# The output projection as seven products over all eight token tiles, with the right blocks summed and split in stage one

## Chip, cores and metric

The kernel runs on one core of a Trainium2 chip. The metric is the device time of one execution in microseconds (us). A profile of one execution goes with it: what each engine did and when. TensorE (PE) does the matmuls, VectorE (DVE) and ScalarE (ACT) the element-wise work, GpSimd (POOL) a little of it, and SyncE's queue (SP) issues nearly all transfers (DMAs).

## What is computed

One layer of a streaming encoder: two attentions from one input projection, gated and merged, an output projection, a layer norm, a gated feed-forward network (FFN) and a second norm. Sequence and model width are 1024, the inner width of the FFN is 2816, everything is float32.

```python
h = x @ w_in[l]
qa, ka, va, qb, kb, vb, ga, gb = jnp.split(h, split_pts, axis=-1)
y_a = chunk_band_attention(heads_a(qa), heads_a(ka), heads_a(va), rel_bias[l]) @ w_proj_a[l]
y_b = stick_breaking_attention(heads_b(qb), heads_b(kb), heads_b(vb)) @ w_proj_b[l]
gate_a = jax.nn.sigmoid(ga + b_gate[l, :D])
gate_b = jax.nn.sigmoid(gb + b_gate[l, D:])
mix = (gate_a * y_a + gate_b * y_b) @ w_out[l]
x = layer_norm(DEEPNORM_ALPHA * x + mix, ln1_g[l], ln1_b[l])
gu = x @ w_ffn_in[l]
g, u = jnp.split(gu, 2, axis=-1)
ffn = (jax.nn.silu(g) * u) @ w_ffn_out[l]
x = layer_norm(DEEPNORM_ALPHA * x + ffn, ln2_g[l], ln2_b[l])
```

## The kernel before

**Products in three parts.** A float32 product a b is made of three fast products: each operand is split into a high part (ScalarE copies it into the type float32r) and a low part (VectorE subtracts the high part from it), and TensorE adds a_h b_h, a_h b_l and a_l b_h. `split` (L109, L110) does one operand, `mm3` (L116 to L119) the three matmuls. Weights are split in the same way by `begin_w` (L550, L551).

**Seven products for eight.** Most big products are cut into 2 x 2 blocks and done with seven block products, as Strassen and Winograd do, so that sums and differences of blocks have to be made of both operands. `run_pairs` runs such units, one after another, seven steps p each; a step is 12 matmuls of 128x512. It prepares the next unit's operands between the steps, calls `aside` after each step and `also` at the unit's end.

**Stages.** (1) The input projection, units 0 to 13, until 333.6 us of the profile; each unit from 6 on lasts some 19 us. `aside_work(i)` puts other work at the end of unit i + 1: `sum_wo(j)` makes four differences of the blocks of w_out (L576 to L579) and stores them to `wt_dr`; `store_proj` splits parts of the projections behind the attentions and stores them. (2) The attentions, 16 heads, until about 640 us: scores (`sc_a`, L705 and L706), a custom VectorE operation that adds the bias and takes the maximum (L748), the exponential on ScalarE (L754), a scaling on GpSimd (L759), transposes on TensorE (`tp_a`, L817), splits, and the products with v (`pv_a`). Between a head's matmuls stand matmuls that wait for nothing there, the fill: first the gate blocks 10 to 15 (`gps`, L606, 24 matmuls for each half of the tokens), then a projection. `FILL` gives their number by head, 18 in the first ones. (3) The second projection, the merge into `mA`, the output projection (`ops`), the first norm, and transposes of its result (`x1ps`, L1209). (4) The two products of the FFN, from 766.7 us on, and the second norm.

**The output projection.** Token tiles 0 to 3 go by seven products of two tiles each (L1369, 7 x 2 x 12 matmuls); tiles 4 to 7 go plainly (through `mm3`, 2 halves x 4 tiles x 24 matmuls). Its weights are loaded after the attentions, w_out's own blocks and the stored differences, and split there (`begin_wo`, 16 tiles of 128x1024). `take_in` adds a finished accumulator to the residual tile `acc` (L1348). `norm_1` is one VectorE chain but for the power: statistics (L1183), their sum (L1186), a power on GpSimd (L1187), scaling (L1188), and the second scaling with the offset ln1_b (L1191).

**What sets the order.** Each engine works through one queue in order. A scheduler of the framework sets these orders at build time from the program's order and its own estimates, but for the instructions that are tied to one another by hand. Tiles live in slots: a tag has so many buffers, and a new tile waits until the old one in its buffer is done with.

```python
SLOTS = dict(bw=9, pt=4, yt=3, qs=2, kh=2, kl=2, v=2, gt=3, kp=4, op=8, xt=16)
BANKS = dict(mm=2, sc=2, tr=3, pv=1)
```

The slots `qs`, `kh`, `kl` and `v` hold a head's queries, keys (high and low) and values during the attentions, and side work's tiles in stage one; `cycle` goes round a list of tags.

## Time and profile before

| | |
|---|---|
| median of 3 runs | 1412.12 us (1411.85 to 1412.22) |
| the profiled execution | 1412.51 us, of which the span on the core is 1410.7 |
| TensorE busy | 1399.7 us, 99%, 6642 matmuls in the trace |
| VectorE, ScalarE, GpSimd busy | 1034.1, 699.0, 236.0 us |
| DMA | 292.28 MB, share of the 16 engines 58.2% |
| granted TensorE clock | 0.999 |

A profile line of a group gives the code line, engine, operation, output and inputs, shapes and count, then the busy time in us and the mean of one in ns, then the engine's idle time before them and what ended it. A line of the chain gives a start and a duration in us and what ran. Idle time of an engine that is not the bottleneck costs nothing.

### The profile page before, as it was taken

The page shows a single profiled execution, that of the slowest core. Times are in us where ns is not written, and L with a number is a line of the kernel's source. Part 1 is how long each engine was busy: PE and PEld are TensorE (multiplying, and loading weights), DVE is VectorE, ACT ScalarE, POOL GpSimd, SP SyncE. Part 2 cuts the span into 40 slices and gives each one's busy share as a digit, 9 for nine tenths or more (in the row PEclk, how much of TensorE's full clock was granted, in tenths as well). Part 3 has the DMA queues.
Part 4 walks back from the last instruction along what each step waited for, and adds up shares of the span by engine and source line. Part 5 has one row for each costly group of instructions (what it writes and reads, how often), then busy time and mean ns, then how long its engine had stood idle before and what let it go on. Part 6 is the DMA issues. An engine that isn't in the chain of part 4 may idle for free.

```text
span 1410.7 us, 18935 instructions
## 1 busy us (share of the span) xinstructions
PE 1399.7 (99%) x6642; PEld 1164.6 (83%) x6642; DVE 1034.1 (73%) x1671; ACT 699.0 (50%) x1245; POOL 236.0 (17%) x308
## 2 busy tenths in 40 slices
PE   9999999999999999999999999999999999999997
PEld 7888888888888888888888888888888888888886
DVE  8967657545887788878998967767677765847666
ACT  6544444545888888774413644434444443322220
POOL 0000000002555878750001000000000000000033
PEclk9999999999999999999999999999999999999999
DMA  7476468856676478755651144433444349996652
GB/s 254 165 286 224 178 236 303 295 179 238 212 231 208 130 252 281 253 198 194 231 202 75 61 148 166 149 141 143 164 164 149 143 144 342 411 385 236 233 194 90
DMA packets 98927, 292.28 MB, mean 207 GB/s; under 512 B 9728, under 2 KB 26112, under 8 KB 98832
## 3 DMA queue, kind: packets, MB, share of 16 engines
q1 hardware_dynamic: 98832, 291.07, 58.2%
q8 instruction: 52, 0.85, 0.3%
q14 instruction: 43, 0.35, 0.1%
HBM read 187.20 MB, written 100.17 MB: 204 GB/s over the span
## 4 chain that ended last, share of the span: by engine, by line
PE 94%; DVE 2%; DMA 1%; ACT 1%; issue 1%; POOL 0%; DVEq 0%; SPq 0%; ACTq 0%; POOLq 0%
PE sxf L179 16%; PE d L1512 15%; PE sxp L179 9%; PE szf L179 8%; PE v L481 5%; PE gps L606 4%; PE szp L179 4%; PE syf L179 4%; PE yAps L910 3%; PE ops L1369 3%; PE syp L179 2%; PE tp_b L817 2%; PE tp_a L817 2%; PE plain L347 1%; PE pv_b L833 1%; PE pv_b L832 1%
## 5 line engine op out<-in xcount | busy, mean ns | idle before, releaser
L1512 PE MATMUL d<-wd,sl 128*128 128x512 f32 (+1 forms) x924 | 207.7, 387 | 0.0
L1512 PEld LDWEIGHTS d<-wd,sl 128*128 128x128 f32 x924 | 172.3, 188 | 35.4
L1532 POOL TENSOR_TENSOR mv<-mv,neghalf 128x1 f32<-128x1 f32 x8 | 9.0, 1121 | 606.7 <-DVE mv L1531 606.7
L109 ACT CAST wd<-wd 128x512 fp32r<-128x512 f32 x77 | 45.9, 621 | 114.1 <-PE d L1512 66.8
L794 POOL TENSOR_TENSOR w_b<-w_b,kp_b 128x511 f32<-128x511 f32 (+3 forms) x96 | 96.0, 1012 | 23.2 <-DVE kp_b L789 16.7
L110 DVE TENSOR_TENSOR sl<-h,sl 128x512 fp32r<-128x512 f32 x77 | 52.6, 686 | 27.6 <-ACT sl L109 27.6
L789 DVE TENSOR_TENSOR_SCAN kp_b<-kp_b,ident_ps 128x512 f32<-128x512 f32 (+2 forms) x64 | 56.5, 885 | 21.0 <-ACT kp_b L786 20.0
L109 ACT CAST sl<-h 128x512 fp32r<-128x512 f32 x77 | 47.5, 620 | 48.1 <-PE syf L179 18.3
L1489 DVE TENSOR_TENSOR x<-d,x 128x512 f32<-128x512 f32 (+1 forms) x41 | 27.6, 675 | 47.6 <-PE d L1512 47.5
L786 ACT ACTIVATE kp_b<-sc_b 128x512 f32<-128x512 f32 (+3 forms) x96 | 48.3, 504 | 28.0 <-PE sc_b L706 23.6
L110 DVE TENSOR_TENSOR wd<-wd,wd 128x512 fp32r<-128x512 f32 x77 | 52.7, 709 | 10.7 <-ACT wd L109 10.6
L179 PE MATMUL szf<-x1S63h,wcf 128*128 128x512 f32 x168 | 55.1, 389 | 0.0
L110 DVE TENSOR_TENSOR pt_b<-tp_b,pt_b 128x512 fp32r<-128x512 f32 (+1 forms) x96 | 49.9, 544 | 6.6 <-ACT pt_b L109 5.7
L729 POOL MEMSET bias<- 64x64 f32 x2 | 0.3, 145 | 314.3 <-ACT bias L725 314.3
L109 ACT CAST pt_b<-tp_b 128x512 fp32r<-128x512 f32 (+1 forms) x96 | 46.6, 503 | 8.0 <-PE tp_b L817 7.6
L759 POOL TENSOR_SCALAR w_a<-w_a,st_a 128x640 f32<-128x640 f32 (+2 forms) x64 | 42.2, 669 | 48.0 <-PE sc_a L706 26.6
L754 ACT ACTIVATE w_a<-w_a,st_a 128x640 f32<-128x640 f32 (+2 forms) x64 | 44.7, 700 | 8.6 <-DVE st_a L748 7.5
L787 ACT ACTIVATE w_b<-sc_b 128x511 f32<-128x511 f32 (+3 forms) x96 | 48.3, 504 | 0.0
L817 PE MATMUL tp_b<-ident,w_b 128*128 128x128 f32 x288 | 47.3, 272 | 0.2
L110 DVE TENSOR_TENSOR pt_a<-tp_a,pt_a 128x512 fp32r<-128x512 f32 (+1 forms) x96 | 44.6, 486 | 3.3 <-ACT pt_a L109 2.2
L1307 ACT ACTIVATE h<-sxf 128x512 f32<-128x512 f32 x21 | 12.6, 598 | 68.2 <-PE sxf L179 68.2
L817 PEld LDWEIGHTS tp_b<-ident,w_b 128*128 128x128 f32 x288 | 36.4, 140 | 11.1 <-DVE pt_b L110 1.1
(1574 smaller groups left out, 4285.2 us busy)
## 6 DMA issues: line engine op xcount, KB each, us to landing
s_dr<-sl SPq DMA_DIRECT2D x77, 512.0 KB, 2.6
sl<-s_dr SPq DMA_DIRECT2D x77, 512.0 KB, 7.6
wLf<-in_w_ffn_in_dram SPq DMA_DIRECT2D x22, 512.0 KB, 4.3
wRf<-in_w_ffn_in_dram SPq DMA_DIRECT2D x22, 512.0 KB, 3.6
wd<-in_w_ffn_out_dram SPq DMA_DIRECT2D x22, 512.0 KB, 8.2
v_dr<-vc SPq DMA_DIRECT2D x16, 512.0 KB, 3.4
qs<-q_dr SPq DMA_DIRECT2D x16, 512.0 KB, 6.7
kh<-k_dr SPq DMA_DIRECT2D x16, 512.0 KB, 6.5
```

The lines of the kernel that those rows point to most:

```text
L109: return (nc.scalar.copy(dst_h, src), nc.vector.tensor_tensor(dst_l, src, dst_h.bitcast(F32), ALU.subtract))
L110: nc.vector.tensor_tensor(dst_l, src, dst_h.bitcast(F32), ALU.subtract))
L179: mm(acc, lw[:, ks], rx, start=(first and kt == i == 0), stop=(kt == 3 and i == 2), skip_group_check=not first)
L481: mm(accs[j], a, b, start=(first and kt == n == 0), stop=(kt == 3 and n == 2), skip_group_check=True)
L606: mm(acc[hf], lw[:, ks], rx[k][:, (LO, HI)[hf]], start=(k == j == 0), stop=(k == KT - 1 and j == 2))
L754: nc.scalar.activation(s[:, 0:w], s[:, 0:w], AF.Exp, bias=st[:, m:m + 1], scale=-1.0, accum_out=st[:, 2:3])
L786: nc.scalar.activation(kp[:, c0:e], sc[:, 0:n], AF.Sigmoid, scale=-1.0)
L787: nc.scalar.activation(be[:, m0:e], sc[:, m0 - c0:n], AF.Sigmoid)
L789: nc.vector.tensor_tensor_scan(kp[:, 0:e], kp[:, 0:e], ident_ps()[:, 0:e], 0.0, ALU.mult, ALU.add)
L794: nc.gpsimd.tensor_tensor(be[:, m0:e], be[:, m0:e], kp[:, m0 - 1:e - 1], ALU.mult)
L817: ins = tr(tp[:, (qb - lo_q) * P:(qb - lo_q + 1) * P], wt[qb - q0][:, (kb - qb) * P:(kb - qb + 1) * P], ident)
L1512: mm(part, a, b, start=(fresh and i == k == 0), stop=(i == n - 1 and k == 2), skip_group_check=not fresh)
```

## The change

All eight token tiles go through the seven products: each of the seven (`OUT`) runs over the four tiles j of a token half, 7 x 4 x 12 matmuls. The seven sums and blocks of w_out are made for one k tile at a time by `sum_wo(kt)`, which now returns seven parts; each does at most one difference, one split and one store of 512 KB to `wo_dr`. They run one after each step of units 7, 9, 11 and 13. `store_proj` comes two at a time. After the attentions the 28 tiles are loaded already split. In the first norm, tiles 0 to 5 leave the second scaling to ScalarE, and their offset ln1_b is added by a transfer that GpSimd issues, from SBUF to SBUF, accumulating; tiles 6 and 7 stay on VectorE. The loads for the FFN's start and the stores of `x1_dr` come later, and the VectorE chain of takes, statistics, norms and some splits is tied in program order. The layout of w_out in memory changes with it, and the helpers of the two norms are merged.

The diff, cut to its core:

```diff
+    WO_AT, PROJ_AT = (6, 8, 10, 12), (5, 7, 9, 11)
+
     def aside_work(i):
         if i == 2:
             small_inputs()
-        if i in (2, 6):
-            sum_wo(i // 6)
-        if i >= len(work) - 9:
-            store_proj(i - len(work) + 9)
+        if i in PROJ_AT:
+            for j in range(2):
+                store_proj(2 * PROJ_AT.index(i) + j)
+        if i + 1 in WO_AT:
+            parts.extend(sum_wo(WO_AT.index(i + 1)))
...
-    wt_dr = {n: dram(f"wt_dr{n}_", 2) for n in ("t1", "t2", "t3", "t4")}
-    wo_src = {n: [w_out[b, j] for j in range(2)] for b, n in enumerate(("11", "12", "21", "22"))}
-
-    def sum_wo(j):
-
-        put, sub = nc.vector.tensor_tensor, ALU.subtract
-        x_, y_, z_, u_ = (cycle(QKV, f"wo{n}r{j}") for n in ("11", "12", "21", "22"))
-        for t, n in ((x_, "11"), (y_, "12"), (u_, "22"), (z_, "21")):
-            dma(t, wo_src[n][j])
-        put(x_, y_, x_, sub)
-        put(y_, u_, y_, sub)
-        put(u_, u_, x_, sub)
-        put(z_, z_, u_, sub)
-        for t, n in ((x_, "t1"), (y_, "t3"), (u_, "t2"), (z_, "t4")):
-            dma(wt_dr[n][j], t)
+    wo_dr = {p: dram(f"wo_dr{p}_", 4) for p in range(1, 8)}
+    parts = []
+
+    def next_part(i):
+        if parts:
+            parts.pop(0)()
+
+    def sum_wo(kt):
+
+        xy, zu = (cycle(("qs", "kh"), f"wo{n}r{kt}") for n in ("xy", "zu"))
+        dma(xy, w_out[kt + 4])
+        dma(zu, w_out[kt])
+        x_, y_, z_, u_ = (t[:, cs] for t in (xy, zu) for cs in (LO, HI))
+
+        def out(p, src, dst=None, in0=None, in1=None):
+            def part():
+                if dst is not None:
+                    nc.vector.tensor_tensor(dst, in0, in1, ALU.subtract)
+                o = cycle(("kl", "v"), f"wo{p}_{kt}", F32R)
+                split(o[:, LO], o[:, HI], src)
+                dma(wo_dr[p][kt], o.bitcast(F32))
+            return part
+
+        return [out(3, u_), out(1, x_), out(5, x_, x_, y_, x_), out(7, y_, y_, u_, y_),
+                out(6, u_, u_, u_, x_), out(2, z_), out(4, z_, z_, z_, u_)]
...
-              right_or_v, first=3, then=rest_of_start, also=aside_work, wide=V_AT - 1, then_right=2)
+              right_or_v, first=3, then=rest_of_start, also=aside_work, aside=next_part,
+              wide=V_AT - 1, then_right=2)
...
+    def load_wo(p):
+        wo[p] = [slot("xt", f"wo{p}_{kt}", F32R) for kt in range(4)]
+        for t, d in zip(wo[p], wo_dr[p]):
+            wo["last"] = dma(t.bitcast(F32), d)
+
+    def m_split(p, kt, src, tie=lambda ins: ins):
+        o = {5: lambda *a: slot("bw", *a), 4: lambda *a: slot("pt", *a)}.get(
+            p, lambda *a: cycle(QKV, *a))(f"m{p}_{kt}", F32R)
+        tie(split(o[:, LO], o[:, HI], src)[1])
+        m_ops[p][kt] = o
+
+    put, sub = nc.vector.tensor_tensor, ALU.subtract
+
+    def m_sums(kt):
+
+        a, b = m_raw[kt + 4], m_raw[kt]
+        m_split(4, kt, b[:, HI])
+        put(b[:, HI], a[:, HI], b[:, HI], ALU.add)
+        m_split(5, kt, b[:, HI])
+        put(a[:, HI], a[:, LO], a[:, HI], sub)
+
+    def m_sums_3(kt):
+        a, b = m_raw[kt + 4], m_raw[kt]
+        put(a[:, LO], b[:, HI], a[:, LO], sub)
+        put(b[:, LO], b[:, LO], a[:, LO], sub)
+        m_split(3, kt, b[:, LO])
 
...
+    def finish(name, n, t, g, b, lone, done, cuts=(slice(0, D),), tied=False, added=None):
...
+            if lone:
+                tie(nc.vector.scalar_tensor_tensor(t[:, cs], t[:, cs], mv[:, 2:3], b[:, cs],
+                                                   ALU.mult, ALU.add))
+            else:
+                nc.scalar.activation(t[:, cs], t[:, cs], AF.Copy, scale=mv[:, 2:3])
+                if added is None:
+                    nc.gpsimd.tensor_tensor(t[:, cs], t[:, cs], b[:, cs], ALU.add)
+                else:
+                    nc.gpsimd.dma_start(t[:, cs], added[:, cs], accum_op=ALU.add)
+            done(cs)
...
     def norm_1(tt):
+        finish(f"1_{tt}", 2, acc_t[tt], g1, b1, tt > 5, lambda cs: None, tied=True, added=b1)
+
+    bx, by = [None] * 4, [None] * 4
+
+    def project_out(p, j):
+        accs = by if p in (2, 5, 3) else bx
         first = p in (1, 2, 5)
+        if first:
+            accs[j] = bank(("tr", "tr", "tr", "pv")[j] if accs is by
+                           else ("mm", "mm", "sc", "sc")[j], f"ops{p}_{j}")
+        for kt in range(4):
+            lh, ll = (m_ops[p][kt][:, c + j * P:c + (j + 1) * P] for c in (0, HW))
+            wh, wl = (wo[p][kt][:, cs] for cs in (LO, HI))
+            for n, (a, b) in enumerate(((lh, wh), (lh, wl), (ll, wh))):
+                mm(accs[j], a, b, start=(first and kt == n == 0), stop=(kt == 3 and n == 2),
+                   skip_group_check=not first)
+        tt, cs = j + 4 * (p in (5, 7, 4)), (LO, HI)[p in (5, 7, 3, 6)]
+        take_in(tt, cs, accs[j], 1.0 if p in (2, 6, 7) else ALPHA)
+        if p in (6, 4):
+            mark(f"1_{tt}", 1, acc_t[tt][:, cs], True)
+        elif p in (2, 7):
+            mark(f"1_{tt}", 0, acc_t[tt][:, cs], p == 7)
+
+    def after_chain(work):
+        with tc.issue_after(wo["last"].ins), tc.issue_after(chained[0].ins):
+            work()
+
+    def start_of_ffn():
+        left_f(0)
+        R0 = slot("gt", "wRf0")
+        dma(R0, w_ffn_in[NF])
+        Wf[0]["hr"] = split_w(R0, "wrf0", "bw")
+
+    for p in OUT[:5]:
+        todo = {1: [lambda: m_sums(last_c), lambda: load_wo(5)], 5: [lambda: load_wo(6)],
+                2: [lambda: load_wo(3)] + [lambda kt=kt: m_sums_3(kt) for kt in range(2)],
+                3: [lambda: load_wo(7)],
+                6: []}[p]
+        if p == 5:
+            todo += [lambda kt=kt: m_sums_3(kt) for kt in (2, 3)]
+        elif p in (3, 6):
+            half = LO if p == 3 else HI
+            todo += [lambda kt=kt: m_split(6 if p == 3 else 7, kt, m_raw[kt + 4][:, half],
+                                           chain)
+                     for kt in range(4)]
+            if p == 6:
+                load_wo(4)
         elif p == 2:
             for _ in range(3):
                 more_acc("yt")
             more_acc("bw")
+        for j in range(4):
+            project_out(p, j)
+            for _ in range(-(-len(todo) // (4 - j)) if p != 6 else 2):
+                if todo:
+                    todo.pop(0)()
+            if p == 6:
+                norm_1(j)
+    for n, (p, j) in enumerate(((7, 0), (7, 1), (4, 0), (7, 2), (4, 1), (7, 3), (4, 2), (4, 3))):
+        project_out(p, j)
+        if p == 4:
+            norm_1(j + 4)
+        if n > 3:
+            x1_operands(0, acc_t, (n - 4,))
+        if n == 4:
+            after_chain(start_of_ffn)
+        elif n == 6:
+            after_chain(lambda: left_f(1))
+    for tt in range(4):
+        dma(x1_dr[tt], acc_t[tt])
+    after_chain(lambda: right_f(1))
+    after_chain(lambda: left_f(2))
 
     first_h = []
 
     def second_half():
         x1_operands(1, acc_t)
+        for tt in range(4, 8):
+            dma(x1_dr[tt], acc_t[tt])
...
```

Three places of the built orders follow. First SyncE's queue at the end of stage one, before. `qs`, `kh`, `kl` are loads for the heads, `g_dr` stores of finished gate blocks (their names end in the unit), `wp_dr` stores of `store_proj`, `braw` loads of the bias:

```order
L685 DMA qs_2626<-q_dr_77 128x1024
L720 DMA braw_2632<-rel_dr 128x640
L591 DMA wp_dr_0_291<-wh_proj_2614 128x1024
L720 DMA braw_2640<-rel_dr 128x640
L395 DMA g_dr_110<-c_12_2445 128x1024
L541 DMA wr_g_2620<-in_w_in_dram 128x1024
L395 DMA g_dr_109<-c_12_2398 128x1024
L591 DMA wp_dr_1_292<-wl_proj_2615 128x1024
L689 DMA kh_2628<-k_dr_85 128x1x1024
L685 DMA qs_2634<-q_dr_77 128x1024
L689 DMA kl_2630<-k_dr_85 128x1x1024
L689 DMA kh_2636<-k_dr_85 128x1x1024
```

And after, with `wo_dr` the stores of `sum_wo` (kt is the number 3 in the name):

```order
L590 DMA wo_dr_3_272<-wo_3_2655 128x1024
L699 DMA qs_2758<-q_dr_77 128x1024
L590 DMA wo_dr_3_280<-wo_3_2637 128x1024
L590 DMA wo_dr_3_288<-wo_3_2674 128x1024
L590 DMA wo_dr_3_296<-wo_3_2693 128x1024
L590 DMA wo_dr_3_292<-wo_3_2711 128x1024
L395 DMA g_dr_112<-c_13_2671 128x1024
L590 DMA wo_dr_3_276<-wo_3_2729 128x1024
L395 DMA g_dr_111<-c_13_2635 128x1024
L590 DMA wo_dr_3_284<-wo_3_2748 128x1024
L703 DMA kh_2760<-k_dr_85 128x1x1024
L703 DMA kl_2762<-k_dr_85 128x1x1024
```

Seven stores of the last k tile now stand ahead of the first `kh`, among them those of the parts that follow unit 13's last steps; the loads of the second head went behind.

Then TensorE's queue at the start of the attentions, before (`sxp` is unit 13's last accumulator):

```order
L179 MATMUL sxp_2513<-xl_196,wbp13h 128x512
L179 MATMUL sxp_2513<-xh_195,wbp13l 128x512
L705 MATMUL sc_a_0_0_2653<-kh_2628,qs_2626 128x320
L706 MATMUL sc_a_0_0_2653<-kl_2630,qs_2626 128x320
L705 MATMUL sc_a_0_1_2657<-kh_2628,qs_2626 128x320
L706 MATMUL sc_a_0_1_2657<-kl_2630,qs_2626 128x320
L606 MATMUL gps_0_2723<-xh_181,wh_g_2622 128x512
L606 MATMUL gps_0_2723<-xl_182,wh_g_2622 128x512
L705 MATMUL sc_a_1_0_2663<-kh_2628,qs_2626 128x320
L706 MATMUL sc_a_1_0_2663<-kl_2630,qs_2626 128x320
```

And after:

```order
L619 MATMUL gps_1_3067<-xh_195,wh_g_2754 128x512
L619 MATMUL gps_1_3067<-xl_196,wh_g_2754 128x512
L619 MATMUL gps_1_3067<-xh_195,wl_g_2755 128x512
L719 MATMUL sc_a_0_0_2785<-kh_2760,qs_2758 128x320
L719 MATMUL sc_a_0_1_2789<-kh_2760,qs_2758 128x320
L720 MATMUL sc_a_0_0_2785<-kl_2762,qs_2758 128x320
L720 MATMUL sc_a_0_1_2789<-kl_2762,qs_2758 128x320
L719 MATMUL sc_a_1_0_2795<-kh_2760,qs_2758 128x320
L720 MATMUL sc_a_1_0_2795<-kl_2762,qs_2758 128x320
L719 MATMUL sc_a_1_1_2799<-kh_2760,qs_2758 128x320
```

The 48 matmuls of gate block 10 (`gps_0` and `gps_1`) have moved from between the scores of heads 0 to 2 to a place ahead of the first score.

Last GpSimd's queue in the first norm, before (`mv` holds a tile's mean and variance):

```order
L1187 TENSOR_TENSOR mv_0_7494<-mv_0_7494,neghalf 128x1
L1187 TENSOR_TENSOR mv_1_7517<-mv_1_7517,neghalf 128x1
L1187 TENSOR_TENSOR mv_2_7542<-mv_2_7542,neghalf 128x1
L1187 TENSOR_TENSOR mv_3_7565<-mv_3_7565,neghalf 128x1
L1187 TENSOR_TENSOR mv_4_7772<-mv_4_7772,neghalf 128x1
```

And after:

```order
L1182 TENSOR_TENSOR mv_0_7693<-mv_0_7693,neghalf 128x1
L1194 DMA acc_7296<-ln1b 128x1024
L1182 TENSOR_TENSOR mv_1_7719<-mv_1_7719,neghalf 128x1
L1194 DMA acc_7298<-ln1b 128x1024
L1182 TENSOR_TENSOR mv_2_7739<-mv_2_7739,neghalf 128x1
L1194 DMA acc_7300<-ln1b 128x1024
L1182 TENSOR_TENSOR mv_3_7759<-mv_3_7759,neghalf 128x1
L1194 DMA acc_7302<-ln1b 128x1024
L1182 TENSOR_TENSOR mv_4_7811<-mv_4_7811,neghalf 128x1
L1194 DMA acc_7425<-ln1b 128x1024
```

Between the powers now stand the accumulating transfers of tiles 0 to 5, each behind ScalarE's scaling of its tile.

More of the change, by code (lines that the diff above doesn't have):

```diff
@@ L1219, in x1_operands @@
                     nc.scalar.copy(part, tps[i])
-                    split(o[:, LO], o[:, HI], part)
+                    chain(split(o[:, LO], o[:, HI], part)[1])
                     ops_1[1 + i].append((o[:, LO], o[:, HI]))
@@ L1342, in next_piece @@
             pieces.pop(0)()
[L1344 removed]
     def take_in(tt, cs, acc, scale=ALPHA):
         t = acc_t[tt][:, cs]
[L1348 to L1349 removed]
+        chain(nc.vector.scalar_tensor_tensor(t, t, scale, acc, ALU.mult, ALU.add))
     def norm_1(tt):
[L1352 to L1356 removed]
+        finish(f"1_{tt}", 2, acc_t[tt], g1, b1, tt > 5, lambda cs: None, tied=True, added=b1)
```

241 lines of the change are left out of this document (53 added, 188 removed).

## Prediction

> **What bounds the kernel now.** I read the page first: busy time per engine, then the chain that ended last. The rows are the span, the busy times, and the chain's shares by engine.
>
> ```profile
> span 1410.7 us, 18935 instructions
> PE 1399.7 (99%) x6642; PEld 1164.6 (83%) x6642; DVE 1034.1 (73%) x1671; ACT 699.0 (50%) x1245; POOL 236.0 (17%) x308
> PE 94%; DVE 2%; DMA 1%; ACT 1%; issue 1%; POOL 0%; DVEq 0%; SPq 0%; ACTq 0%; POOLq 0%
> ```
>
> TensorE has work for 1399.7 of 1410.7 us, and the chain is TensorE's. Next I read the table of TensorE's waits; its rows give line waited for, total, number, longest. Two stand for seven.
>
> ```profile
> PE warm L266 <- DVE warm L263: 1.2, 1, 1.2
> PE tp_a L817 <- DVE pt_a L110: 0.3, 1, 0.3
> ```
>
> The longest wait of the run is 1.2 us, at the start. So only fewer matmuls can win time, and every wait the change puts in front of TensorE is a pure loss. The chain then gives the price of a matmul: the first row lies in stage one, the second is the seven-product part of the old output projection.
>
> ```profile
> 325.64 2.72 PE sxp L179 x12
> ...
> 681.64 38.08 PE ops L1369 x168
> ```
>
> 38.08 / 168 = 0.2267 us each, the same as 2.72 / 12.
>
> **The matmuls removed.** The old projection has 168 matmuls in seven products and 2 x 4 x 24 = 192 plain ones; the new one has 7 x 4 x 12 = 336. That is 24 fewer: 24 x 0.2267 = 5.44 us won, all on the path, because nothing else sets the end there. The rest of the sum is what TensorE loses elsewhere.
>
> **The sums of w_out in stage one.** The table by stretches gives span, TensorE, weight loads, VectorE, ScalarE and GpSimd busy (with counts), the granted clock, the DMA share. Rows: units 7, 9, 11 and 13, whose products now carry the parts of `sum_wo`.
>
> ```profile
> 200.00:219.00 19.00, 19.00 (x85) 15.76 (x84) 12.66 (x16) 8.16 (x10) 0.00 (x0) 1.00 0.82 304
> 238.00:257.00 19.00, 19.00 (x85) 15.58 (x84) 12.74 (x15) 11.70 (x14) 0.00 (x0) 1.00 0.90 330
> 276.00:295.00 19.00, 19.00 (x86) 15.73 (x85) 10.07 (x12) 9.79 (x12) 0.00 (x0) 1.00 0.53 194
> 314.00:333.60 19.60, 19.60 (x88) 16.25 (x87) 4.43 (x5) 5.15 (x7) 0.29 (x2) 1.00 0.89 306
> ```
>
> And the prices of a split half, a split whole, and ScalarE's copy of a half:
>
> ```profile
> L110 DVE TENSOR_TENSOR x1A<-x1raw,x1A 128x512 fp32r<-128x512 f32 x8 | 5.3, 682 | 0.0
> L551 DVE TENSOR_TENSOR wl_proj<-wr_proj,wh_proj 128x1024 fp32r<-128x1024 f32 x8 | 9.8, 1221 | 9.4 <-DMA g_dr<-c 5.3 <-ACT wh_proj L550 4.1
> L109 ACT CAST x1A<-x1raw 128x512 fp32r<-128x512 f32 x8 | 4.6, 636 | 0.0
> ```
>
> One k tile costs VectorE 4 differences and 7 low parts of 128x512: 11 x 0.69 = 7.6 us, and ScalarE 7 x 0.64 = 4.5. By the new order unit 9 is the fullest: 12.7, less two old differences and one split of w_proj (3 x 1.22), plus 8 of k tile 1's eleven (5.5) and four half-tile operations that move there from unit 10 (2.8): 17.3 of 19 us. The matmuls hide this as long as VectorE takes each finished accumulator in time; at nine tenths, in one queue behind loads and slots, it can slip by some tenths. SP carries 32 more transfers in all; in stage one 36 of 512 KB in place of 16, at a share of already 0.90 in unit 9. Between nothing and one whole difference per loaded unit (4 x 0.7 = 2.8) I take 0.3, near the low end, since the units between have room.
>
> **The start of attention.** This is the large term. The seventh part of k tile 3 comes after unit 13's last product, and its raw tile and outputs stand in the slots of `qs`, `kh`, `kl` and `v`. Before, these loads were out in units 12 and 13; the views by tile give (for `qs`, then `kh`) first and last issue, and `kh`'s landing time.
>
> ```profile
> L685 SPq DMA_DIRECT2D qs<-q_dr x2: 438/812/1187, 301.2 to 319.3; - x2
> L689 SPq DMA_DIRECT2D kh<-k_dr x3: 534/557/651, 318.6 to 341.2; - x3
> DMA to landing us min/median/max: 4.6/5.6/6.7
> ```
>
> Now `kh` for head 0 stands on SP behind the last two stores of `sum_wo`. Unit 13's last product ends at 333.6; ScalarE takes it (0.6) and splits part six (0.62), VectorE does its low part, the last difference and, after another ScalarE copy (0.62), the last low part (3 x 0.69): 337.5. `kh` goes out at about 337.9, `kl` 0.55 later, and they land at 342.5 to 345.1. TensorE has gate block 10 in front of the scores now, 48 x 0.2267 = 10.9 us, until 344.5. So the loads come in just in time: 0 to 0.6, I take 0.
>
> The price is that the 48 matmuls are gone from heads 0 to 2, whose chains they covered. Rows: the stretches up to the first score of head 0, and to the first bias operation of heads 1, 2 and 3; the three forms of the gate matmuls in them; and, from the chain and the timeline, the first score, VectorE's first pass over it and the first transpose.
>
> ```profile
> 333.60:342.70 9.10, 8.97 (x49) 6.93 (x49) 6.41 (x31) 7.38 (x15) 3.99 (x6) 1.00 0.59 190
> 342.70:358.60 15.90, 15.90 (x103) 13.92 (x101) 13.23 (x50) 13.97 (x40) 8.26 (x12) 1.00 0.55 179
> 358.60:373.20 14.60, 14.60 (x95) 13.05 (x94) 11.77 (x46) 11.82 (x32) 9.29 (x12) 1.00 0.59 177
> ...
> L606 PE MATMUL gps<-xh,wh_g 128*128 128x512 f32 x17 | 7.1, 420 | 0.0
> L606 PE MATMUL gps<-xh,wl_g 128*128 128x512 f32 x16 | 7.1, 443 | 0.0
> L606 PE MATMUL gps<-xl,wh_g 128*128 128x512 f32 x16 | 7.1, 442 | 0.0
> ...
> 333.64 0.30 PE L705 MATMUL sc_a<-kh,qs 128*128 128x320 f32 x1
> 334.25 0.49 DVE L748 CUSTOM_DVE_ANT_0 w_a<-sc_a,bias 128x320 f32<-128x320 f32 x1 [2.44 <-PE sc_a L706]
> 339.54 0.33 PE tp_a L817
> ```
>
> Of these 39.6 us some 48 gate matmuls are 10.9, so the heads' own TensorE work is 28.7. In the new order the three heads get only about 6 others (1.4), so without waits head 3 would begin at 344.5 + 28.7 + 1.4 = 374.6. VectorE's share of the three stretches is 6.41 + 13.23 + 11.77 = 31.4 us and can't begin before the first bias is made. ScalarE's queue has the copy of gate block 10 and then the bias ahead of it:
>
> ```profile
> L611 ACT COPY gate<-gps 128x512 f32<-128x512 f32 x3 | 1.8, 602 | 0.0
> L725 ACT ACTIVATE bias<-braw 128x640 f32<-128x640 f32 x4 | 2.9, 730 | 0.0
> L729 POOL MEMSET bias<- x2: 145/145/145, 312.9 to 316.0; 64x64 f32 x2
> ```
>
> 344.5 + 0.6 + 0.73 + 2 x 0.15 = 346.2. Lower bound: VectorE without a gap from there, 346.2 + 31.4 = 377.6, a loss of 3.0 us. Upper bound: the heads keep their old pace though the cover is gone, 346.2 + (373.2 - 334.25) = 385.2, a loss of 10.6, and 11.2 with the late loads. In the old stretches VectorE is busy 81 to 83% of the time beside a full TensorE; without fill I put it at 93%, nearer the full end since TensorE then answers at once: 346.2 + 33.8 = 380.0, a loss of 5.4. From head 3 on (13, 17, 18 fill matmuls) nothing more is lost.
>
> **The end of the projection.** Rows: VectorE's take of a half tile, its statistics, their sum, its scaling, GpSimd's power, a ScalarE pass of 128x1024; then the transfers nearest to the new accumulating ones.
>
> ```profile
> L1348 DVE SCALAR_TENSOR_TENSOR acc<-acc,ops 128x512 f32<-128x512 f32 x22 | 14.6, 681 | 4.4 <-PE ops L1369 3.3 <-PE ops L119 1.1
> L1183 DVE BATCH_NORM_STATS2 bn<-acc 128x6 f32<-128x512 f32 x15 | 10.0, 687 | 0.2
> L1186 DVE BATCH_NORM_AGGREGATE mv<-bn 128x2 f32<-128x12 f32 x7 | 1.4, 207 | 0.2
> L1188 DVE SCALAR_TENSOR_TENSOR acc<-acc,mv,ln1g 128x1024 f32<-128x1024 f32 x7 | 9.1, 1298 | 0.2
> L1187 POOL TENSOR_TENSOR mv<-mv,neghalf 128x1 f32<-128x1 f32 x7 | 6.2, 886 | 134.0 <-DVE mv L1186 134.0
> L109 ACT CAST wlf0h<-wLf 128x1024 fp32r<-128x1024 f32 x1 | 1.1, 1052 | 5.3 <-DMA wLf<-in_w_ffn_in_dram 5.3
> ...
> s_dr<-sl SPq DMA_DIRECT2D x77, 512.0 KB, 2.6
> wd<-in_w_ffn_out_dram SPq DMA_DIRECT2D x22, 512.0 KB, 8.2
> ```
>
> Call E the end of product 6 on tile 3. VectorE still has tile 2's sum and scaling (1.5) and then tile 3's take, statistics, sum and scaling (2.9): E + 4.4, with the splits queued between up to E + 6.9. Product 7 on tile 0 is taken after that (0.7), at E + 5.1 to 7.6, and product 4 on tile 0 needs its bank at E + 28 x 0.2267 = 6.3: a wait of 0 to 1.3, I take 0.4. The first transposes of x1 come 60 matmuls after E, at E + 13.6, and need tile 3 whole: ScalarE's scaling (1.05) ends at E + 5.4 to 7.9, then the accumulating transfer, between 2.6 and 8.2 us by the nearest rows (a store, and the slowest load): E + 8.0 to 16.1, a wait of 0 to 2.5. I take 0.5. Together 0.9.
>
> [...]
>
> What vanishes besides (VectorE's 16 splits of 128x1024 weights after attention, and tiles 0 to 5's second scalings) was under full matmuls, and its cover stays: nothing gained.
>
> **The sum.** 1412.51 (the profiled execution, span 1410.7 plus 1.8 around it; the runs' median is 1412.12, 0.4 lower) - 5.4 + 0.3 + 5.4 + 0.9 = 1413.7. My forecast is 1413.7 us.
>
> **Rivals.** First: the cover wasn't needed. Heads 0 to 2 run at VectorE's pace and lose 3.0 or less, the rest nothing: 1412.5 - 5.4 + 1.6 (0 to 3) = 1408.7 (1407 to 1410). For it speaks that VectorE's queue is nearly all of a head; against it the waits on ScalarE and GpSimd inside each head. Second, slower: the accumulating transfers are late. GpSimd's queue alternates power and transfer, so a transfer that holds it delays the next tile's power too, and tile 3 is the fourth. The first could go out three tiles (3 x 2.72) before E + 7.9, at E - 0.3. At 5 us each, about midway between 2.6 and 8.2, one behind the other, the fourth lands at E + 19.7, and the first x1 transpose waits 6.1 for it: 1413.7 - 0.5 + 6.1 = 1419.3 (1416.5 to 1422). It decides from 3.5 us each on (4 x 3.5 - 0.3 = 13.7). Against it: a transfer needn't hold the queue until it lands. [...] Third, slower: the old pace stays in heads 0 to 2, with loads late on SP, at the upper bound: 1412.5 - 5.4 + 11.2 + 0.9 = 1419.2 (1417 to 1421). It decides from a loss of 8 there.
>
> **How the numbers follow.** Forecast (1410 to 1416.5) 0.48, cover not needed 0.26, transfers late 0.12, old pace 0.14. Within 0.2% means 1409.3 to 1414.9, about what a measurement can tell from no change. The forecast gives 0.04 to faster, 0.36 to same and 0.08 to slower. Faster: 0.26 + 0.04 = 0.30; same 0.36; slower 0.08 + 0.12 + 0.14 = 0.34. The range goes from 1407.0 (a start that costs nothing) to 1420.0, and leaves out the outer parts of the last two cases and the little that lies below.
>
> **What would show it.** The projection's matmuls would be 336 of 0.227 us, 76.2 us. TensorE would have new waits: 4 to 7 us in all on ScalarE, VectorE and GpSimd between 344 and 381, first `sc_a` against `bias` or `kl`; some tenths at product 4 on tile 0 against VectorE; and, if at all, at the first `x1ps` against the transfer `acc<-ln1b`. Unit 13 would end at about 334. I am wrong if heads 1 and 2 last under 12.5 us each with TensorE hardly waiting, or if stage one ends more than 1 us late.

## The result, and the profile after

| | before | after |
|---|---|---|
| median | 1412.17 us (1411.85 to 1412.26) | 1444.08 us (1442.49 to 1445.39) |
| the profiled execution | 1412.51, span 1410.7 | 1444.32, span 1442.5 |

The ratio is 1.0226 (95% interval 1.0208 to 1.0244): slower by 2.3%, 31.9 us, and far outside the range forecast. From the profile page of after, the span, the busy times and the chain's shares by engine:

```profile
span 1442.5 us, 19048 instructions
PE 1406.9 (98%) x6618; PEld 1165.6 (81%) x6618; DVE 1037.9 (72%) x1694; ACT 704.6 (49%) x1262; POOL 241.1 (17%) x314
PE 87%; DVE 5%; DMA 3%; ACT 2%; issue 2%; POOL 1%; SPq 0%; DVEq 0%; ACTq 0%; POOLq 0%
```

TensorE has 24 matmuls less and yet 7.2 us more busy time, and it is idle for 35.6 us of the span, 24.6 more than before. So there are two losses to look for: waits, and matmuls that take longer. TensorE's waits of 1.0 us and more in all (line, what it waited for, total, number, longest), but for the old 1.2 of `warm`:

```profile
PE sxp L179 <- ACT c L207: 5.7, 2, 5.1
PE syf L179 <- DVE h L1276: 3.7, 1, 3.7
PE sxp L179 <- ACT c L198: 3.3, 2, 3.1
PE tp_a L831 <- POOL w_a L773: 2.8, 4, 1.6
PE sxf L179 <- ACT gt L198: 2.4, 1, 2.4
PE x1ps L1207 <- DMA acc<-ln1b: 1.8, 1, 1.8
PE plainhl_512f L116 <- ACT gt L1275: 1.2, 1, 1.2
...
PE sc_a L719 <- DVE st_a L762: 1.1, 1, 1.1
PE szp L179 <- ACT c L211: 1.0, 1, 1.0
```

The first, third and last rows are in stage one (`sxp`, `szp` are its accumulators), the fourth and eighth at the start of the attentions, the rest at the end of the projection and the start of the FFN. To place the whole loss I took four moments from the views by tile, in us:

| | before | after | lost in between |
|---|---|---|---|
| stage one ends | 333.6 | 346.8 | 13.2 |
| first `ops` (projection starts) | 681.5 | 705.3 | 10.6 |
| first matmul of the FFN (`plainhl`) | 766.7 | 787.4 | -3.1 |
| first `d` (second FFN product) | 1193.0 | 1224.2 | 10.5 |

13.2 + 10.6 - 3.1 + 10.5 = 31.2 of the 31.8 us between the spans; 0.6 are behind the last `d`.

**Stage one.** Nearly all of it is lost in two waits of TensorE in unit 9: 3.1 us that end at 252.9, and 5.1 us that end at 263.8. First the chain of waits in after (start, duration, what ran), then ScalarE's timeline (in brackets its idle time before the instruction, and what ended it), then SyncE's:

```profile
249.23 4.93 DMA wr_proj<-in_w_proj_dram
...
254.22 1.06 ACT wh_proj L553
...
255.31 1.24 DVE wl_proj L554
...
257.22 5.32 DMA woxyr<-in_w_out_dram
...
263.76 4.95 PE sxp L179 x11
```

```profile
252.28 0.58 ACT L198 COPY c<-sxp 128x512 f32<-128x512 f32 x1 [3.42 <-DMA wp_dr<-wl_proj]
...
262.61 0.62 ACT L109 CAST wo<-woxyr 128x512 fp32r<-128x512 f32 x1 [3.10 <-DMA woxyr<-in_w_out_dram]
263.13 0.58 ACT L207 COPY c<-sxp 128x512 f32<-128x512 f32 x1
```

```profile
250.94 0.44 SPq L141 DMA_DIRECT2D wRp<-in_w_in_dram  x1
255.30 0.33 SPq L604 DMA_DIRECT2D wp_dr<-wh_proj  x1
256.56 0.33 SPq L604 DMA_DIRECT2D wp_dr<-wl_proj  x1
257.22 0.33 SPq L580 DMA_DIRECT2D woxyr<-in_w_out_dram  x1
```

The first wait is one for a slot. The copy that frees TensorE's accumulator needs a buffer that still holds a low part of w_proj, and ScalarE waits 3.42 us until the store of that part (`wp_dr<-wl_proj`) has landed. The splits of w_proj, the sums with their raw tiles, and the finished results `c` and `hi` of the projection all go round the slots of `qs`, `kh`, `kl` and `v`.

The second wait is a long hand-over through SP's queue. A raw block of w_proj lands (4.93 us), and ScalarE and VectorE split it. SP works in order and issues nothing from 251.4 to 255.3, because the store of the high part is next and isn't ready. The load of `woxyr`, the raw tile of w_out, stands behind both stores. Its slot does not hold it up: in the built program the tile before it in that buffer is a finished block of keys, whose store was issued at 244.91 and took 2.7 us to land. The load lasts 5.32 us. ScalarE's cast of it stands in its queue ahead of the copy that frees TensorE's accumulator, so ScalarE stands idle for 3.10 us in front of a finished accumulator, and TensorE waits 5.1 us. The last chain row shows the second loss: 11 matmuls took 4.95 us, not 2.5. Stretches there (columns as in the prediction):

```profile
261.80:268.80 7.00, 5.04 (x13) 4.03 (x14) 3.23 (x5) 2.27 (x5) 0.00 (x0) 0.53 0.71 282
269.00:270.00 1.00, 1.00 (x6) 0.81 (x5) 0.84 (x2) 1.00 (x2) 0.00 (x0) 1.00 0.00 0
```

The granted clock is a half from 261.6 to 268.4, beginning inside the pause, and then 1.00 again; in before it is 1.00 through all of stage one. The fall came 2.9 us into the pause, which begins at 258.7, and of these 6.8 us the last 3.4 are busy throughout. TensorE is busy at half clock from 263.8 to 268.4, 4.7 us. The waits of stage one sum to 10.0 us; with half of these 4.7 that is 12.3 of the 13.2.

**The start of the attentions.** A row of the chain and a stretch of after, then a stretch of before that begins at its first score:

```profile
346.82 10.89 PE gps L619 x48
```

```profile
357.50:397.00 39.50, 34.35 (x190) 27.69 (x190) 29.36 (x121) 31.58 (x80) 19.95 (x30) 0.91 0.74 240
```

```profile
333.60:386.00 52.40, 52.27 (x322) 44.94 (x322) 41.79 (x163) 43.74 (x109) 27.33 (x35) 1.00 0.64 202
```

The 48 gate matmuls run at full pace ahead of the first score, as forecast. Then TensorE is idle for 39.5 - 34.35 = 5.2 us, and the half clock from 360.6 to 367.4 is up to 3.4 more: 8.6 of 10.6. From 397 to 412 TensorE is busy without a gap again.

**The start of the FFN.** Two stretches of 20.2 us that end at the first `h`, before and after, and then after's from its first FFN matmul on:

```profile
775.40:795.60 20.20, 20.11 (x95) 16.36 (x94) 20.13 (x30) 15.05 (x24) 0.00 (x0) 1.00 0.01 1
```

```profile
804.50:824.70 20.20, 13.63 (x62) 10.40 (x60) 20.20 (x30) 14.90 (x24) 0.00 (x0) 0.92 0.00 1
787.40:832.00 44.60, 36.45 (x167) 28.82 (x165) 42.87 (x59) 26.23 (x40) 2.46 (x2) 0.92 0.20 68
```

VectorE is busy without a gap in both, nearly all of it with differences and low parts of the normed x; after's stretch also holds a weight split of 1.22 us (`wlf2`) that before did at 745. In before TensorE had enough to do beside it; in after it runs out and stands idle for 44.6 - 36.45 = 8.2 us from its first FFN matmul on.

**The projection.** The group of the projection's matmuls and a row of the chain inside them; then the accumulating transfers in 750 to 800 (KB each, and the median until landing), and the one that TensorE waits for, in the chain:

```profile
L1359 PE MATMUL ops<-wo,m 128*128 128x512 f32 x336 | 77.5, 391 | 0.0
```

```profile
705.50 46.26 PE ops L1359 x204
```

```profile
acc<-ln1b POOLq DMA_DIRECT2D x6, 512.0 KB, 7.6
```

```profile
767.72 8.22 DMA acc<-ln1b
```

### The profile page after: what moved, and what is told of

The parts are those of the page before. It is cut to its first block, busy times and chain, and to the rows that moved or that the text cites. A ratio compares the mean times of both kernels' runs of the same rounds, so it can differ in the third digit from the quotient of the medians.

```text
span 1442.5 us, 19048 instructions
## 1 busy us (share of the span) xinstructions
PE 1406.9 (98%) x6618; PEld 1165.6 (81%) x6618; DVE 1037.9 (72%) x1694; ACT 704.6 (49%) x1262; POOL 241.1 (17%) x314
## 4 chain that ended last, share of the span: by engine, by line
PE 87%; DVE 5%; DMA 3%; ACT 2%; issue 2%; POOL 1%; SPq 0%; DVEq 0%; ACTq 0%; POOLq 0%
PE sxf L179 15%; PE d L1510 14%; PE szf L179 8%; PE sxp L179 8%; PE v L481 5%; PE gps L619 4%; PE syf L179 4%; PE ops L1359 4%; PE szp L179 3%; PE yAps L924 3%; PE tp_b L831 2%; PE tp_a L831 2%; PE syp L179 2%; PE plain L347 2%; PE pv_b L847 1%
## 5 line engine op out<-in xcount | busy, mean ns | idle before, releaser
L1182 POOL TENSOR_TENSOR mv<-mv,neghalf 128x1 f32<-128x1 f32 x16 | 17.3, 1080 | 732.7 <-DVE mv L1181 732.6
L1359 PE MATMUL ops<-wo,m 128*128 128x512 f32 x336 | 77.5, 391 | 0.0
L1359 PEld LDWEIGHTS ops<-wo,m 128*128 128x128 f32 x336 | 62.8, 188 | 13.4 <-DVE acc L1342 0.4
L110 DVE TENSOR_TENSOR pt_a<-tp_a,pt_a 128x512 fp32r<-128x512 f32 (+1 forms) x96 | 44.6, 486 | 4.1 <-ACT pt_a L109 3.1
L831 PE MATMUL tp_a<-ident,w_a 128*128 128x128 f32 x240 | 44.0, 278 | 3.2 <-POOL w_a L773 2.8
```

The source lines that it names most:

```text
L110: nc.vector.tensor_tensor(dst_l, src, dst_h.bitcast(F32), ALU.subtract))
L831: ins = tr(tp[:, (qb - lo_q) * P:(qb - lo_q + 1) * P], wt[qb - q0][:, (kb - qb) * P:(kb - qb + 1) * P], ident)
L1359: mm(accs[j], a, b, start=(first and kt == n == 0), stop=(kt == 3 and n == 2), skip_group_check=not first)
```

## The experiments

For each loss the question is which part of the change makes it. Stage one first: the sums alone, the pairs of `store_proj` alone, or both through the shared slots?

**The sums left out.** The loads after the attentions read stored parts of w_proj in place of the sums.

```diff
-        if i + 1 in WO_AT:
-            parts.extend(sum_wo(WO_AT.index(i + 1)))
...
-        for t, d in zip(wo[p], wo_dr[p]):
+        for t, d in zip(wo[p], [wp_dr[p][kt % 2] for kt in range(4)]):
```

> The changed kernel without the sums of w_out in stage one: no loads, differences, splits and stores of sum_wo; the projection then reads 28 stored tiles of w_proj in place of the sums, so its values are not the layer's, while its matmuls, loads and norms are unchanged. Theory: the 13.2 us lost in stage one and the 10.5 us lost at the start of the attentions both come from the sums. Then stage one ends at about 333.6 us again, the first score follows directly, and the time is 1444.1 - 13.2 - 10.5 = 1420.4 (1418 to 1423). Rival: pairing the splits of w_proj is the cause of stage one's part; then stage one still ends after 340 and the time is above 1428.

Measured: 1421.11 us (1420.17 to 1421.33), ratio 1.006 (1.0045 to 1.0075). The first score starts at 332.8, the first `ops` at 680.5: both earlier than before. The time is where the theory put it. So without `sum_wo` all of the loss up to the projection is gone, 23.8 us, and the 8.9 that remain lie behind it. The pairs of `store_proj` alone cost nothing.

**The w_proj splits one at a time again.** As many bytes and operations, but no pair ahead of the sums in the slots.

```diff
-        if i in PROJ_AT:
-            for j in range(2):
-                store_proj(2 * PROJ_AT.index(i) + j)
+        if i >= len(work) - 9:
+            store_proj(i - len(work) + 9)
```

> The changed kernel with the splits of w_proj one at the end of each unit, as before, and all else as changed. Theory A (slots and queues): the pair of w_proj splits holds the slots that the raw tiles of the sums wait for, the loads come late, and ScalarE's casts of the sums stand waiting ahead of the copies that free TensorE's banks. Then stage one's loss falls from 13.2 to under 5 us and the time to 1432 to 1437. Theory B (transfers): the 10 MB more in stage one at a DMA share of 0.9 and over are the cause; the bytes are the same here, so stage one ends at 345 to 349 again and the time stays within 3 us of 1444.

Measured: 1434.91 us (1433.19 to 1436.55), ratio 1.0159 (1.0144 to 1.0174). Stage one ends at 335.4: it lost 1.8 in place of 13.2, with all the sums in and as many bytes moved, so theory B is out. But the attentions now lose 12.5. Its waits and a stretch:

```profile
PE sc_a L718 <- DMA kh<-k_dr: 3.3, 1, 3.3
...
PE sxp L179 <- ACT c L207: 1.4, 1, 1.4
```

```profile
350.00:357.00 7.00, 6.24 (x17) 3.96 (x18) 3.83 (x16) 2.76 (x7) 0.67 (x1) 0.50 1.07 384
```

The loads of the first head stand on SP behind the last stores: the first `kh` goes out at 342.5, 7.1 us after the end of stage one, in after 4.4. TensorE waits 3.3 us for it and then has 10.2 us at half clock. That is the late `kh` that the forecast took as 0.

**No w_proj splits at all.** The second projection reads stored sums in place of them.

```diff
-        if i in PROJ_AT:
-            for j in range(2):
-                store_proj(2 * PROJ_AT.index(i) + j)
...
-        for d, t in zip(wp_dr[4 * br + cc], hl):
+        for d, t in zip(wo_dr[1 + cc][2 * br:2 * br + 2], hl):
```

> The changed kernel with its sums of w_out but without the splits of w_proj in stage one (their readers read stored sums, so the values are not the layer's). Theory A (shared slots): the sums alone find the slots free, stage one loses under 2 us of its 13.2, while the loss at the start of the attentions stays between 5 and 11 us, since the last sums still follow unit 13's products: 1427 to 1433. Theory C (the sums' own work on ScalarE and VectorE or their own transfers): stage one loses 8 us or more as now, above 1437.

Measured: 1430.07 us (1428.7 to 1432.57), ratio 1.0125 (1.0108 to 1.0142). Stage one loses 2.8, a little over theory A's 2, the attentions 6.2 (with a wait of 2.5 for `kh`). With the first run, either kind of side work alone costs at most 2.8 in stage one, both in pairs 13.2: the cost is that of the two meeting, not of the work. In after's trace they meet in a slot (the wait of 3.1) and in SP's order (the wait of 5.1); no run changes one of these and leaves the other.

**The last k tile one unit earlier.** This is to give the heads' loads their slots in time.

```diff
-    WO_AT, PROJ_AT = (6, 8, 10, 12), (5, 7, 9, 11)
+    WO_AT, PROJ_AT = (6, 8, 10, 11), (5, 7, 9, 11)
```

> The changed kernel with the sums of the last k tile in unit 12 in place of unit 13. Theory: the start of the attentions loses 10.5 us because the last sums keep the slots and SyncE's queue that the first heads' loads need; with them a unit earlier the loads go out in time, gate block 10 stays among the scores of heads 0 to 2, and at least 8 of the 10.5 us come back: 1434 to 1437, if stage one loses no more than now. Rival: the heads lose their time because stage one ran late as a whole (stores and loads behind it); then nothing changes, 1442 to 1446.

Measured: 1445.86 us (1445.74 to 1446.08), ratio 1.0237 (1.022 to 1.0254). The time forecast was missed, since stage one now loses some 23 us, in these waits:

```profile
PE sxp L179 <- ACT c L198: 5.8, 4, 3.1
PE szp L179 <- ACT c L211: 4.4, 2, 3.4
PE sxp L179 <- ACT c L207: 4.1, 1, 4.1
```

But the gate matmuls stand among the scores again, and from the end of stage one to the first `ops` about 1 us is lost, not 10.6.

**Both edits.** One w_proj split at a time, and the last k tile at 11.

```diff
-    WO_AT, PROJ_AT = (6, 8, 10, 12), (5, 7, 9, 11)
+    WO_AT, PROJ_AT = (6, 8, 10, 11), (5, 7, 9, 11)
...
+        if i >= len(work) - 9:
+            store_proj(i - len(work) + 9)
```

> The changed kernel with single splits of w_proj at each unit's end (as before) and the last k tile's sums in unit 12 in place of 13. Theory: stage one loses by the slots that pairs and sums share (single splits bring its loss from 13.2 to about 2), the attentions by the first heads' loads behind the last sums (10.5 to 12.5). Both together: 1434.9 less some 10 = 1425 (1421 to 1429), first score below 340 us. Rival: sums in unit 12 and w_proj splits until the end of unit 13 keep each other's slots, as in the run with the last k tile early, and the loss only moves from the heads into units 12 and 13: 1433 or more.

Measured: 1441.85 us (1441.14 to 1442.83), ratio 1.0206 (1.0191 to 1.0221): the rival held. The two merely meet elsewhere; in its chain, at 304, the same hand-over stands as in after at 249, now inside unit 12. Here too SP waits, 3.4 us, for a cast of w_proj, with the load of `woxyr` behind:

```profile
304.31 4.62 DMA wr_proj<-in_w_proj_dram
...
311.67 5.21 DMA woxyr<-in_w_out_dram
```

**The sums early.** Single splits, and the k tiles much earlier, so that nothing of them stands near the heads.

```diff
-    WO_AT, PROJ_AT = (6, 8, 10, 12), (5, 7, 9, 11)
+    WO_AT, PROJ_AT = (2, 3, 6, 8), (5, 7, 9, 11)
```

(and `store_proj` as in the second run)

> The changed kernel, the whole layer, with the sums of w_out in units 3, 4, 7 and 9 in place of 7, 9, 11 and 13, and single splits of w_proj. Theory: the last sums are then out of the slots long before the first heads' loads, so the attentions start as before; stage one, where only units 7 and 9 share slots with w_proj splits, loses up to 4 us; what remains is the 8.9 us of the kernel without the sums: 1421 to 1425. If the early units are as tight, stage one loses more and the time is above 1428.

Measured: 1430.0 us (1429.63 to 1431.08), ratio 1.0125 (1.0109 to 1.014). The attentions lose 0.3 and have no wait: their loss comes from the place of the last sums. Stage one loses 10.6, earlier: TensorE waits twice for ScalarE's copies `vc`, 6.0 us in all, the longer time (3.3) between 126 and 134, where VectorE has no gap.

```profile
126.00:134.00 8.00, 4.67 (x15) 3.46 (x14) 8.00 (x12) 6.57 (x12) 0.00 (x0) 0.79 0.83 330
```

Next the end of the projection and the start of the FFN. From the first `ops` to the first `d` before takes 511.5 us; 24 matmuls less would be 506.1; after takes 518.9. The sums are left out in most of these runs, so that nothing ahead disturbs.

**FFN weights early.** The loads and splits of the FFN's start go ahead of products 7 and 4.

```diff
+                after_chain(start_of_ffn)
...
-        if n == 4:
-            after_chain(start_of_ffn)
-        elif n == 6:
+        if n == 2:
             after_chain(lambda: left_f(1))
```

(with the raw tiles of `left_f(0)` and of `R0` in the slots of `op`)

> The changed kernel with the first FFN weights (left and right block 0) loaded and split from product 6 on and left block 1 from product 7 on, their raw tiles in other slots. Theory: the 10.8 us lost at the start of the FFN are a backlog on VectorE, which is busy without a gap from 803 to 839 us; three splits of 1.22 us taken out of it win at least 3.7 us and part of what the slower clock costs there: 1436 to 1440. Rival: the late accumulating transfers and with them the late transposes of x1 set it; then at most 1 us is won, 1443 to 1445.

> The kernel without the sums (1421.1 us), with the first FFN weights split from product 6 on as in the run before that did so on the changed kernel. There the split of the left block and of the right block did leave the last stretch (3 x 1.22 us) and the time fell by 1.9 us only. Theory A: VectorE's backlog after the last product falls by some 2 us of it, and 1 to 3 us are won: 1418 to 1420. Theory B (it makes no difference, what counts is VectorE's 18 us after the last x1 transposes, which nothing here shortens): 1420.5 to 1422.

The first of the two, measured on after: ratio 1.0208 (1.0191 to 1.0225), about 2.5 us less than after, where the theory wanted at least 3.7. But from the first `ops` to `d` it is 518.7, no gain: the 2.5 lie ahead of the edit's place. The second, with the sums out: 1418.72 us (1417.23 to 1420.99), 2.4 less than without the edit, but 520.3 against 521.0 in the profiled executions. Inconclusive: when the FFN's weights come matters by a us or two, and in neither profile does it remove the waits for `h` (3.5 and 3.5).

**The first norm's first scaling left out** (on the kernel without sums), 8 VectorE operations of 1.29 us.

```diff
-            tie(nc.vector.scalar_tensor_tensor(t[:, cs], t[:, cs], mv[:, 0:1], g[:, cs],
-                                               ALU.subtract, ALU.mult))
+            if name[0] == "2":
+                tie(nc.vector.scalar_tensor_tensor(t[:, cs], t[:, cs], mv[:, 0:1], g[:, cs],
+                                                   ALU.subtract, ALU.mult))
```

> The kernel without the sums (1421.1 us), and the first norm leaves out VectorE's first scaling (mean and ln1_g) on all eight tiles, 8 x 1.3 us, 4 x 1.3 of them in the last product; the values are not the layer's. Theory A (VectorE's backlog): the last x1 transposes come 3 to 5 us earlier, the waits at the start of the FFN (7.0 us in all) shrink to under 3, and with the clock 5 to 8 us are won: 1413 to 1416. Theory B (accumulating transfers): the transfers only start 1.3 us earlier each, 1 to 2 us are won: 1419 to 1420.

**The sums of the FFN's second right block left out** (on the kernel without sums), VectorE work between the last norm and `h`.

```diff
     def right_f(f):
+        if f == 1:
+            Wf[1]["R"] = slot("gt", "wRf1")
+            dma(Wf[1]["R"], w_ffn_in[NF + 1])
+            Wf[1]["ha"] = Wf[1]["hb"] = Wf[1]["hl"]
+            return
```

> The kernel without the sums (1421.1 us), and the FFN's right block 1 isn't summed and split: its products read the left block's parts, so the values are not the layer's; 5.2 us of VectorE's work between the last norm and the first FFN sums go (four of 0.68, two of 1.22). Theory A: from the last norm (771.9) to h (800.6) VectorE works without a gap, so h comes some 5 us earlier, the waits there (7.0 us) shrink to 2 or less, and with the clock 5 to 8 us are won: 1413 to 1416. Theory B (a wait for a transfer or for ScalarE sets h): under 2 us, 1419 to 1421.

**Both left out.** The two edits together:

```diff
+            if name[0] == "2":
...
+            Wf[1]["ha"] = Wf[1]["hb"] = Wf[1]["hl"]
```

> The kernel without the sums, without the first scaling in the first norm and without the sums and splits of the FFN's right block 1 (values not the layer's): 15.6 us less on VectorE from product 6 to the first FFN sums. Theory A: VectorE sets the way from the projection to the FFN, so with enough of its work gone the 24 matmuls show: 1412.4 - 5.4 = 1407 plus the wait for the accumulating transfer (1.6 to 2.3): 1406.5 to 1410. Theory B: something else holds the FFN back, and the time stays above 1412.

Measured: without the first scaling 1417.66 us (1416.27 to 1419.09), 3.45 less than the kernel without sums, between the theories (5 to 8, and 1 to 2); without the right block's sums 1416.84 (1416.43 to 1417.97), 4.3 less, just outside the 1413 to 1416 expected; without both 1413.45 (1411.88 to 1414.46), 7.7 less, which is their sum, but 3.5 above the upper end of theory A and in theory B's range: something besides VectorE is left, as shown below. Taking work from VectorE, with TensorE's queue as it is, gives back 7.7 of the 8.9 us. The second edit also takes two casts of 1.06 us from ScalarE. But in the kernel without sums VectorE works 27.3 of the 28.7 us between the last norm and the first `h` (in before 20.3 of 23.2), so a wait for another engine can't be more than 1.4 of it. So VectorE sets most of what this stretch loses. Two rows show where it stands, the last norm's last operation in before and in the kernel without sums:

```profile
770.34 1.28 DVE L1191 SCALAR_TENSOR_TENSOR acc<-acc,mv,ln1b 128x1024 f32<-128x1024 f32 x1 [0.44 <-POOL mv L1187]
```

```profile
770.59 1.29 DVE L1185 SCALAR_TENSOR_TENSOR acc<-acc,mv,ln1b 128x1024 f32<-128x1024 f32 x1 [0.45 <-POOL mv L1180]
```

Without sums the projection's last matmul starts at 763.6, in before at 766.5: TensorE is 2.9 us earlier, VectorE 0.25 later. What `h` needs of VectorE then still lies ahead, and more of it: `h` starts at 794.8 in before, at 800.6 there, at 794.2 with both left out. Why even then nothing is won shows in two stretches from `ops` to `d`, before and with both left out:

```profile
681.60:1193.00 511.40, 511.31 (x2285) 422.73 (x2284) 383.05 (x531) 220.61 (x328) 7.79 (x8) 1.00 0.44 160
```

```profile
680.90:1194.00 513.10, 508.59 (x2261) 419.31 (x2260) 363.05 (x519) 220.12 (x332) 10.03 (x14) 1.00 0.48 170
```

24 matmuls less should lower TensorE's busy time by 5.4; it falls by 2.7. The half clock from 795.1 to 798.5 explains up to 1.7 of the difference. And 4.5 us are idle: 1.5 before the first `x1ps`, 1.2 for `gt`, 0.8 and 0.3 for `x1A`, 0.7 for `h`. So the 5.4 are used up.

**The offset added by GpSimd in place of transfers** (on the kernel without sums).

```diff
-        finish(f"1_{tt}", 2, acc_t[tt], g1, b1, tt > 5, lambda cs: None, tied=True, added=b1)
+        finish(f"1_{tt}", 2, acc_t[tt], g1, b1, tt > 5, lambda cs: None, tied=True)
```

> The kernel without the sums (1421.1 us), and tiles 0 to 5 of the first norm get their offset by an addition on GpSimd (2.61 us for 128x1024 in the second norm) in place of an accumulating transfer. The sums stay left out, so the values are not the layer's. Theory A: the start of the FFN is late by VectorE's backlog behind the last norms; then only the 2.3 us go that the first x1 transpose waits for the transfer, and perhaps some clock after it: 1418 to 1420.5. Theory B: the accumulating transfers set the start of the FFN (tile 5's lands last before the second transposes); then most of the 8.5 us that the FFN starts late go: 1412 to 1416. If GpSimd's additions hold VectorE up instead, above 1422.

Measured: 1425.52 us (1425.03 to 1427.2), ratio 1.0093 (1.0076 to 1.011), 4.4 more than with transfers, the last of the three cases. GpSimd's additions, a VectorE group beside them, and the same group without the edit:

```profile
L1190 POOL TENSOR_TENSOR acc<-acc,ln1b 128x1024 f32<-128x1024 f32 x6 | 16.4, 2735 | 9.9 <-ACT acc L1188 9.9
```

```profile
L110 DVE TENSOR_TENSOR m<-gA,m 128x512 fp32r<-128x512 f32 x2 | 3.5, 1777 | 0.0
```

```profile
L110 DVE TENSOR_TENSOR m<-gA,m 128x512 fp32r<-128x512 f32 x2 | 1.3, 680 | 0.0
```

Beside the additions these two splits, with two inputs in SBUF, take a mean of 1777 ns, without them 680. The statistics, with one input, take 695 ns with the additions and 694 without. What passes between the two engines no row here shows. So the transfers are the better of the two ways here, 1421.11 against 1425.52 us, though they are not free: with them the first `x1ps` waits 2.3 us.

No run was faster than before. The parts don't add up to one either: without any sums, with the FFN's weights early, 1418.72 us is still above 1412, and every version that computes the layer has the sums to place as well. The best of these is the kernel with early sums, 1430.0.

## Why the prediction was wrong, point by point

**The matmuls removed: right.** 77.5 us busy for 336 against 76.2 forecast; 204 of them in one row of the chain make 46.26 / 204 = 0.2268 us each. But a gain on TensorE counts only while TensorE sets the end, and the forecast took for granted that it does so everywhere, from the page's 99%.

**Stage one, 0.3 forecast (0 to 2.8), 13.2 measured: the step that failed most.** It counted VectorE's work in the unit (17.3 of 19 us) and found room, and named "one queue behind loads and slots" only as some tenths. What it left out is what stands before what. Three kinds of tiles go round `qs`, `kh`, `kl` and `v`, so a copy that frees an accumulator can wait for the store of a w_proj part (3.1 us of TensorE). And SP's one queue holds a load of w_out back behind stores that wait for a load and a split of w_proj. ScalarE's order turns that late load into a stall of TensorE (5.1 us), because a cast that waits for it stands ahead of the copy that frees the accumulator. The sign "stage one ends more than 1 us late" was named as proof against the forecast, and it came.

**The start of the attentions, 5.4 forecast (3.0 to 11.2), 10.6 measured: the mechanism right, a term missing.** The gate block went ahead of the scores, and the cover of heads 0 to 2 was missing; with the last k tile one unit earlier, and with the early sums, the block stays among the scores, and the loss is about 1 and 0.3. The forecast let the three heads take 33.8 us from VectorE's first pass over head 0 to its first over head 3, with VectorE at 93%. In after they take 37.85, near the old 38.95. But after has half clock in these heads, and the run without any w_proj splits has none there. First after, then that run:

```profile
359.45:397.30 37.85, 33.59 (x187) 27.45 (x188) 29.62 (x123) 30.19 (x79) 19.95 (x28) 0.91 0.72 229
348.54:382.68 34.14, 32.75 (x200) 26.98 (x200) 29.63 (x123) 28.43 (x77) 20.09 (x26) 1.00 0.58 188
```

At full clock the heads take 34.1, with the same VectorE work (87% busy). So the forecast's pace was about right, and what it left out is the clock: half for 6.8 of the 37.85 us. The rival "old pace" (14%) comes near after's time, but by luck. Loads "just in time" held in after (0.3 for `kl`); in the runs with single and without w_proj splits `kh` is waited for 3.3 and 2.5 us.

**The end of the projection, 0.9 forecast; 2.3 measured** (-3.1 + 5.4). The wait at the first `x1ps` was 1.8, in the range of 0 to 2.5, against 0.5 taken. Landing took a median of 7.6 us, near the upper row (8.2, a slow load), not the lower. The rival "transfers late" fell as a mechanism: at 7.6 us each, one behind the other, the wait would have been 4 x 7.6 - 0.3 - 13.6 = 16.5. After the first three transfers in after (at 757.4, 761.7 and 764.7) GpSimd's next power started 0.6 to 1.2 us behind the issue, and the transfers overlap: the first four go out 3.0 to 4.3 us apart and none lands in under 5.6.

**"Its cover stays: nothing gained": the second step that failed, 10.5 us.** The forecast freed VectorE of work under full matmuls and asked no further. It didn't ask what VectorE's queue looks like behind the projection. In before it was already full from 775.4 to 795.6 (20.13 of 20.2 us), with the first `h` at its end and TensorE just covered. Taking 5.4 us of matmuls away ahead of it, and moving weight splits from before the last norm to behind it, uncovers it. The runs that leave VectorE's work out show it as the limit: 3.45, 4.3, and together 7.7 us.

**The clock, not in the forecast.** After has three stretches of 6.8 us at half clock, each beginning in or right behind a pause. TensorE is busy in 4.7, 6.5 and 3.2 us of them, so they cost up to 2.3, 3.2 and 1.6. A wait was priced at its length; here some cost their length and up to these 1.6 to 3.2 us on top.

So two of the three losses above 10 us, 13.2 and 10.5, stood at 0.3 and 0. All rivals were built on the attentions and the transfers; none had the slots and SP's order of stage one or VectorE's backlog in it, and so the range could not hold the time. The signs that would show it wrong were well chosen; the bounds were not.

## What to carry to other kernels

When side work is put into slots that others go round, write down for each slot who holds it before and after, and follow each copy and load back through the store that frees its slot; busy shares show nothing of this. On every engine that works in order, look what stands behind an instruction that waits: here on SP a load behind a store that wasn't ready went out late (nothing was issued from 251.4 to 255.3), and on ScalarE a copy that frees an accumulator, behind a cast that waited 3.10 us for that load, passed the wait on to TensorE (5.1 us). Before matmuls are taken away, look in the stretches behind them for an engine with no gap (here VectorE, 20.13 of 20.2 us): there the gain ends, and what was just covered becomes a wait.
